# A sliding-window copy: load order of the channel quarters, eight split stores instead of twelve, one tile for each store buffer

## Chip, cores, metric

One core of one Trainium2 chip; the other cores are idle. The metric is the device time of one execution in microseconds (us), lower is better. Fast runs have a granted clock of 1.0; ratios use fast runs alone. The span of the profile is about 1.8 us shorter than the device time.

## The reference, cut to what matters

```python
x: (16, 64, 64, 64) float32; window 8, stride 4; n_h = n_w = 15
for i in range(15):
    for j in range(15):
        result[:, i, j] = x[:, :, 4*i : 4*i + 8, 4*j : 4*j + 8]   # (16, 15, 15, 64, 8, 8)
```

There is no arithmetic, only movement: 16.78 MB are read, 58.98 MB are written.

## The kernel before

The image is held in `L` on 128 partitions: partition = batch (16) x channel half (2) x quarter of the rows (4), 32 channels in each. A "window" is one column j and one slot s of the four row positions in a quarter; ScalarE (ACT) gathers its 8x8 patches into a buffer, and GpSimd (POOL) stores the buffer with one indirect DMA of 128 rows of 8 KB. For s = 3 the patch crosses into the next partition, so VectorE (DVE) does it with a copy and a shuffle, and one row in four has no place in the output (its index is out of range).

To start storing while loads still run, the first windows are split: their first 16 channels are stored as soon as the first half of the channels is loaded (rows of 4 KB), the others later.

```python
    NCH = 4
    cw = CL // NCH
    for k in range(NCH):                    # 4 parts of the channels x 4 quarters = 16 loads of 1 MB
        for q in range(HQ):
            (nc.sync, nc.scalar)[q % 2].dma_start(
                out=L[q::HQ, k * cw : (k + 1) * cw, :, :],
                in_=x_v[q, :, k * cw : (k + 1) * cw, :])
    # ... cut: index tiles idx, idx_last, idx_h, idx_hlast (h: half rows; last: s = 3)
    UNITS = 18                              # half buffers
    G = gpool.tile([P, UNITS * HCL, WS, WS], f32, name="G")

    def window(j, s, half):
        # ... cut: u, n = place and number of half buffers, cs = the channels
        g = G[:, u * HCL : (u + n) * HCL, :, :]
        if not last:
            nc.scalar.copy(out=g, in_=L[:, cs, s * ST : s * ST + WS, cols])
        else:
            nc.vector.tensor_copy(out=g[:, :, 0:ST, :], in_=L[:, cs, s * ST : RB, cols])
            nc.vector.stream_shuffle(out=g[:, :, ST:WS, :], in_=L[:, cs, 0:ST, cols], mask=nxt)
        st = nc.gpsimd.indirect_dma_start(out=o, out_offset=..., in_=g..., ...)

    EARLY = 12
    for j, s in order[:EARLY]:
        window(j, s, 0)                     # first halves
    while late:                             # then 2 second halves, 2 whole windows, ...
        for w in late[:2]: window(*w, 1)
        for w in rest[:2]: window(*w, None)
        late, rest = late[2:], rest[2:]
    for w in rest: window(*w, None)
```

Of the kernel before, what the change touches and what calls it, by code (L numbers as in the profile page):

```python
# [1 line left out]

# [4 lines left out]


@with_exitstack  # L10
def kernel(
    ctx: ExitStack,
    tc: tile.TileContext,
    x: bass.AP,
    window_size: int,
    stride: int,
    out: bass.AP,
):
    nc = tc.nc
    P = nc.NUM_PARTITIONS  # L20

    B, C, H, W = x.shape
    Bo, NH, NW, Co, WSo, WSo2 = out.shape
    WS = int(window_size)
    ST = int(stride)
    assert Bo == B and Co == C and WSo == WS and WSo2 == WS

    f32 = mybir.dt.float32
    i32 = mybir.dt.int32
    ALU = mybir.AluOpType  # L30
    HQ = 4
    CH = P // (B * HQ)
    CL = C // CH
    RB = H // HQ
    NSLOT = RB // ST
    NWIN = NH * NW
    CFREE = CL * WS * WS
    assert HQ == 4 and CH == 2 and WS == 2 * ST

    lpool = ctx.enter_context(tc.tile_pool(name="lpool", bufs=1))  # L40
    ipool = ctx.enter_context(tc.tile_pool(name="ipool", bufs=1))
    gpool = ctx.enter_context(tc.tile_pool(name="gpool", bufs=1))


    L = lpool.tile([P, CL, RB, W], f32)
    x_v = x.rearrange("b (ch cl) (hq r) w -> hq (b ch) cl (r w)", ch=CH, hq=HQ)
    NCH = 4
    cw = CL // NCH
    for k in range(NCH):
        for q in range(HQ):  # L50
            (nc.sync, nc.scalar)[q % 2].dma_start(
                out=L[q::HQ, k * cw : (k + 1) * cw, :, :],
                in_=x_v[q, :, k * cw : (k + 1) * cw, :],
            )


    def itile(name):
        return ipool.tile([P, 1], i32, name=name)

    pi, tb, tq, tc_, idx, idx_last = (itile(n) for n in ("pi", "tb", "tq", "tc", "idx", "idx_last"))  # L60
    nc.gpsimd.iota(pi[:, :], pattern=[[0, 1]], base=0, channel_multiplier=1)  # L61
    nc.vector.tensor_scalar(out=tb[:, :], in0=pi[:, :], scalar1=3, scalar2=None, op0=ALU.logical_shift_right)  # L62
    nc.vector.tensor_scalar(out=tc_[:, :], in0=pi[:, :], scalar1=2, scalar2=1, op0=ALU.logical_shift_right, op1=ALU.bitwise_and)  # L63
    nc.vector.tensor_scalar(out=tq[:, :], in0=pi[:, :], scalar1=HQ - 1, scalar2=None, op0=ALU.bitwise_and)  # L64
    nc.vector.tensor_scalar(out=tb[:, :], in0=tb[:, :], scalar1=float(NWIN * CH), scalar2=None, op0=ALU.mult)  # L65
    nc.vector.tensor_tensor(out=tb[:, :], in0=tb[:, :], in1=tc_[:, :], op=ALU.add)  # L66
    nc.vector.tensor_scalar(out=tc_[:, :], in0=tq[:, :], scalar1=float(NSLOT * NW * CH), scalar2=None, op0=ALU.mult)  # L67
    nc.vector.tensor_tensor(out=idx[:, :], in0=tb[:, :], in1=tc_[:, :], op=ALU.add)  # L68

    nc.vector.tensor_scalar(out=tq[:, :], in0=tq[:, :], scalar1=float(HQ - 1), scalar2=float(2 * B * NWIN * CH), op0=ALU.is_equal, op1=ALU.mult)  # L70
    nc.vector.tensor_tensor(out=idx_last[:, :], in0=idx[:, :], in1=tq[:, :], op=ALU.add)  # L71


    HCL = CL // 2
    idx_h, idx_hlast = itile("idx_h"), itile("idx_hlast")
    for d, e in ((idx_h, idx), (idx_hlast, idx_last)):
        nc.vector.tensor_scalar(out=d[:, :], in0=e[:, :], scalar1=2.0, scalar2=None, op0=ALU.mult)  # L77
    o_v = out.rearrange("b i j (ch cl) r w -> (b i j ch) (cl r w)", ch=CH)
    o_h = out.rearrange("b i j (ch cl) r w -> (b i j ch) (cl r w)", ch=2 * CH)
    nxt = [min(p + 1, 31) for p in range(32)]  # L80


    UNITS = 18
    G = gpool.tile([P, UNITS * HCL, WS, WS], f32, name="G")
    at = 0

    def window(j, s, half):
        nonlocal at
        cols = slice(j * ST, j * ST + WS)
        last = s == NSLOT - 1  # L90
        if half is None:
            n, c0 = 2, 0
            at += at % 2
        else:
            n, c0 = 1, half * HCL
        u = at % UNITS
        at += n
        cs = slice(c0, c0 + n * HCL)
        g = G[:, u * HCL : (u + n) * HCL, :, :]
        if not last:  # L100
            nc.scalar.copy(out=g, in_=L[:, cs, s * ST : s * ST + WS, cols])  # L101
        else:
            nc.vector.tensor_copy(out=g[:, :, 0:ST, :], in_=L[:, cs, s * ST : RB, cols])  # L103
            nc.vector.stream_shuffle(out=g[:, :, ST:WS, :], in_=L[:, cs, 0:ST, cols], mask=nxt)  # L104
        if half is None:
            o, ix = o_v, (idx_last if last else idx)
        else:
            o, ix = o_h, (idx_hlast if last else idx_h)
        st = nc.gpsimd.indirect_dma_start(  # L109
            out=o,  # L110
            out_offset=bass.IndirectOffsetOnAxis(ap=ix[:, 0:1], axis=0),
            in_=g.rearrange("p c r w -> p (c r w)"),
            in_offset=None,
            element_offset=(s * NW + j) * CH * CFREE + (half or 0) * HCL * WS * WS,
            bounds_check=B * NWIN * CH * (1 if half is None else 2) - 1,
            oob_is_err=False,
        )
        tc.declare_no_dep(st.ins, group="stores", reason="each store writes rows of its own")
        tc.add_to_no_dep_group("stores", st.ins)

    order = [(j, s) for j in range(NW) for s in range(NSLOT)]
    EARLY = 12
    for j, s in order[:EARLY]:
        window(j, s, 0)
    late = list(order[:EARLY])
    rest = list(order[EARLY:])
    while late:
        for w in late[:2]:
            window(*w, 1)
        for w in rest[:2]:  # L130
            window(*w, None)
        late, rest = late[2:], rest[2:]
    for w in rest:
        window(*w, None)


# [1 line left out]
_INS = ['x', 'window_size', 'stride']  # L138
_OUTS = [((16, 15, 15, 64, 8, 8), 'float32')]

_NUMBERS = {'window_size': 8, 'stride': 4}


# [26 lines left out]
```

## Time and profile before

| | before |
|---|---|
| device time, median of 6 runs | 194.41 us (194.27 to 194.75) |
| span of the profile | 192.4 us |
| ACT, POOL, DVE busy | 45%, 37%, 16% of the span |
| first store issued; last load landed | 27.4 us; 49.6 us |
| last data of the faster eight DMA engines; of the slower eight | 184.9 us; 188.6 us |

Read the last two rows as the two ends of the DMA work: before the first store only loads move, and after about 184.9 us half of the DMA engines have nothing left. The rows "landed" and "last data" are from the completion records of the transfers: each store counts a semaphore up sixteen times, once per engine. For the last store, the eighth and the sixteenth count are the ends of the two halves. The lines of the profile are shown in the prediction.

One more line of the page of before is that of a half store: how many, and the median time from issue to landing.

```profile
out_dram<-G,idx_h POOLq DMA_INDIRECT x18, 13.6
```

A half store takes about 1.2 us of the engines' time; 13.6 us means that it stands in a queue behind other work.

### The profile page before, as it was taken

The numbers are of one execution on the slowest core, as the hardware profiler recorded it, in microseconds if no ns is written. First come the engines' busy times: TensorE is split into PE (matmuls) and PEld (weight loads), VectorE is DVE, ScalarE is ACT, GpSimd is POOL, SyncE is SP. The second block draws the span as 40 slices with busy tenths as digits, with TensorE's granted clock in tenths as the row PEclk, the third lists the DMA queues.
The fourth block names the chain that finished last, engine by engine and source line by source line (L and its number), as shares of the span: only waits on it lengthen the run. The fifth ranks groups of instructions, "written<-read, shape, count | busy, mean of one in ns | idle before, by whom it ended". The sixth has DMA issues, their size and how long they took to land.

```text
span 192.4 us, 478 instructions
## 1 busy us (share of the span) xinstructions
DVE 30.4 (16%) x65; ACT 86.2 (45%) x55; POOL 70.3 (37%) x77
## 2 busy tenths in 40 slices
DVE  2000050000232302303030122121121203030000
ACT  0000049500699875373747465646565655600000
POOL 0000027723367766456363253434343434440000
DMA  5999999999999999999999999999999999999960
GB/s 183 418 413 410 410 410 414 417 417 422 420 421 427 429 414 429 404 403 418 412 409 409 419 404 409 416 405 409 409 412 409 409 411 412 407 409 414 424 257 17
DMA packets 14724, 75.80 MB, mean 394 GB/s; under 512 B 1984, under 2 KB 1984, under 8 KB 8960
## 3 DMA queue, kind: packets, MB, share of 16 engines
q0 software_dynamic: 10368, 58.99, 75.3%
q1 hardware_dynamic: 2176, 8.39, 11.0%
q10 hardware_dynamic: 2176, 8.39, 10.8%
q14 instruction: 4, 0.03, 0.0%
HBM read 16.78 MB, written 62.91 MB: 414 GB/s over the span
## 4 chain that ended last, share of the span: by engine, by line
DMA 65%; issue 19%; ACT 3%; POOL 1%; POOLq 1%; PEldq 0%
DMA out_dram<-G,idx_last 38%; DMA out_dram<-G,idx 14%; DMA out_dram<-G,idx_h 8%; DMA out_dram<-G,idx_hlast 6%; ACT G L101 3%; POOL out_dram L109 1%; POOLq L165 1%; POOLq L109 0%; POOL pi L61 0%; PEldq L165 0%
## 5 line engine op out<-in xcount | busy, mean ns | idle before, releaser
L101 ACT COPY G<-L 128x2048 f32<-128x2048 f32 (+1 forms) x54 | 84.9, 1613 | 54.4 <-DMA out_dram<-G,idx 18.6
L109 POOL DMA_INDIRECT out_dram<-G,idx x36 | 34.8, 966 | 47.0 <-DMA out_dram<-G,idx 43.1
L103 DVE COPY G<-L 128x1024 f32<-128x1024 f32 (+1 forms) x18 | 11.1, 618 | 138.3 <-DMA out_dram<-G,idx 62.8
L109 POOL DMA_INDIRECT out_dram<-G,idx_h x18 | 17.4, 966 | 13.9 <-DMA out_dram<-G,idx_hlast 4.3
L104 DVE STREAM_SHUFFLE G<-L 128x1024 f32<-128x1024 f32 (+1 forms) x18 | 19.6, 1090 | 0.0
L109 POOL DMA_INDIRECT out_dram<-G,idx_hlast x6 | 5.9, 990 | 27.9 <-DVE G L104 26.4
L109 POOL DMA_INDIRECT out_dram<-G,idx_last x12 | 11.8, 986 | 11.7 <-DVE G L104 6.8
L101 ACT ACT_TABLE_LOAD x1 | 1.3, 1283 | 26.6 <-DMA L<-in_x_dram 26.6
L62 DVE TENSOR_SCALAR tb<-pi 128x1 int32<-128x1 int32 x1 | 0.2, 155 | 1.0 <-POOL pi L61 1.0
L61 POOL IOTA pi<- 128x1 int32 x1 | 0.1, 120 | 0.4 <-PEq L165 0.4
L104 DVE LOAD_MASK_SELECT G<-L x18 | 0.2, 14 | 0.0
L151 POOL MEMSET const-float32-0.0<- 128x1 f32 x1 | 0.1, 100 | 0.2 <-issue 0.2
L68 DVE CUSTOM_DVE_ANT_0 idx<-tb,tc 128x2 uint16<-128x2 uint16 x1 | 0.2, 160 | 0.0
L66 DVE CUSTOM_DVE_ANT_0 tb<-tb,tc 128x2 uint16<-128x2 uint16 x1 | 0.2, 159 | 0.0
L67 DVE TENSOR_SCALAR tc<-tq 128x1 int32<-128x1 int32 x1 | 0.2, 154 | 0.0
L77 DVE TENSOR_SCALAR idx_hlast<-idx_last 128x1 int32<-128x1 int32 x1 | 0.2, 154 | 0.0
L77 DVE TENSOR_SCALAR idx_h<-idx 128x1 int32<-128x1 int32 x1 | 0.2, 154 | 0.0
L71 DVE CUSTOM_DVE_ANT_0 idx_last<-idx,tq 128x2 uint16<-128x2 uint16 x1 | 0.2, 153 | 0.0
L65 DVE TENSOR_SCALAR tb<-tb 128x1 int32<-128x1 int32 x1 | 0.2, 152 | 0.0
L70 DVE TENSOR_SCALAR tq<-tq 128x1 int32<-128x1 int32 x1 | 0.1, 148 | 0.0
L64 DVE TENSOR_SCALAR tq<-pi 128x1 int32<-128x1 int32 x1 | 0.1, 145 | 0.0
L63 DVE TENSOR_SCALAR tc<-pi 128x1 int32<-128x1 int32 x1 | 0.1, 144 | 0.0
(3 smaller groups left out, 0.3 us busy)
## 6 DMA issues: line engine op xcount, KB each, us to landing
L<-in_x_dram ACTq DMA_DIRECT2D x8, 1024.0 KB, 21.1
L<-in_x_dram SPq DMA_DIRECT2D x8, 1024.0 KB, 19.8
out_dram<-G,idx POOLq DMA_INDIRECT x36, 18.2
out_dram<-G,idx_h POOLq DMA_INDIRECT x18, 13.6
out_dram<-G,idx_last POOLq DMA_INDIRECT x12, 18.3
out_dram<-G,idx_hlast POOLq DMA_INDIRECT x6, 13.1
```

The lines of the kernel that those rows point to most:

```text
L62: nc.vector.tensor_scalar(out=tb[:, :], in0=pi[:, :], scalar1=3, scalar2=None, op0=ALU.logical_shift_right)
L65: nc.vector.tensor_scalar(out=tb[:, :], in0=tb[:, :], scalar1=float(NWIN * CH), scalar2=None, op0=ALU.mult)
L66: nc.vector.tensor_tensor(out=tb[:, :], in0=tb[:, :], in1=tc_[:, :], op=ALU.add)
L67: nc.vector.tensor_scalar(out=tc_[:, :], in0=tq[:, :], scalar1=float(NSLOT * NW * CH), scalar2=None, op0=ALU.mult)
L68: nc.vector.tensor_tensor(out=idx[:, :], in0=tb[:, :], in1=tc_[:, :], op=ALU.add)
L71: nc.vector.tensor_tensor(out=idx_last[:, :], in0=idx[:, :], in1=tq[:, :], op=ALU.add)
L77: nc.vector.tensor_scalar(out=d[:, :], in0=e[:, :], scalar1=2.0, scalar2=None, op0=ALU.mult)
L101: nc.scalar.copy(out=g, in_=L[:, cs, s * ST : s * ST + WS, cols])
L103: nc.vector.tensor_copy(out=g[:, :, 0:ST, :], in_=L[:, cs, s * ST : RB, cols])
L104: nc.vector.stream_shuffle(out=g[:, :, ST:WS, :], in_=L[:, cs, 0:ST, cols], mask=nxt)
L109: st = nc.gpsimd.indirect_dma_start(out=o, out_offset=bass.IndirectOffsetOnAxis(ap=ix[:, 0:1], axis=0), in_=g.rearrange("p c r w -> p (c r ...
L165: with _tile.TileContext(nc) as tc:
```

## The change

The intent: with fewer split stores there are fewer small packets and fewer instructions; since one quarter (third of four, not needed by the first half) is loaded ahead, the first half stores start later, and only one quarter of the loads is left to be covered by them. Separate tiles make each store buffer a tile of its own for the dependency tracking.

```diff
-    for k in range(NCH):
+    for k in (2, 0, 1, 3):
...
-    G = gpool.tile([P, UNITS * HCL, WS, WS], f32, name="G")
+    G = [gpool.tile([P, 2 * HCL, WS, WS], f32, name=f"G{n}") for n in range(UNITS // 2)]
...
-        g = G[:, u * HCL : (u + n) * HCL, :, :]
+        g = G[u // 2][:, u % 2 * HCL : (u % 2 + n) * HCL, :, :]
...
-    EARLY = 12
+    EARLY = 8
```

More of the change, by code (lines that the diff above doesn't have):

```diff
@@ L80 @@
     nxt = [min(p + 1, 31) for p in range(32)]
+    order = [(j, s) for j in range(NW) for s in range(NSLOT)]
     UNITS = 18
-    G = gpool.tile([P, UNITS * HCL, WS, WS], f32, name="G")
+    G = [gpool.tile([P, 2 * HCL, WS, WS], f32, name=f"G{n}") for n in range(UNITS // 2)]
     at = 0
@@ L119, in window @@
         tc.add_to_no_dep_group("stores", st.ins)
-    order = [(j, s) for j in range(NW) for s in range(NSLOT)]
-    EARLY = 12
+    EARLY = 8
     for j, s in order[:EARLY]:
```

## The prediction

> **What bounds the kernel now.** I read the slices of the span first, then the stretches, then the waits and the order in time. The slices say which resource is full:
>
> ```profile
> DMA  5999999999999999999999999999999999999960
> GB/s 183 418 413 410 410 410 414 417 417 422 420 421 427 429 414 429 404 403 418 412 409 409 419 404 409 416 405 409 409 412 409 409 411 412 407 409 414 424 257 17
> ...
> q0 software_dynamic: 10368, 58.99, 75.3%
> q1 hardware_dynamic: 2176, 8.39, 11.0%
> q10 hardware_dynamic: 2176, 8.39, 10.8%
> ```
>
> No slice from the second to the thirty-eighth is below 403 GB/s: loads run into stores with no hole. The bytes are 8.39 + 8.39 = 16.78 MB of loads and 58.99 MB of stores, 75.77 MB. At 411 GB/s that is 184.4 us. The first packet starts at about 2.3 us (packet records), so even full DMA engines would end at 186.7 us; the last packet ends at 188.3 us in those records, and some 4 us of completion and closing follow to the span's 192.4. The stretches show the tail and a small difference in rate (columns: stretch, length, DVE, ACT and POOL busy, clock, DMA share, GB/s):
>
> ```profile
> 2.30:30.00 27.70, 3.00 (x10) 3.40 (x4) 2.08 (x2) 1.00 1.02 405
> 30.00:50.00 20.00, 0.20 (x1) 6.75 (x8) 9.66 (x10) 1.00 1.03 418
> 50.00:80.00 30.00, 7.56 (x16) 24.90 (x18) 18.60 (x19) 1.00 1.02 421
> 80.00:100.00 20.00, 3.99 (x9) 11.29 (x6) 10.66 (x12) 1.00 1.02 410
> 100.00:182.00 82.00, 14.47 (x22) 39.86 (x21) 28.96 (x30) 1.00 1.01 411
> ```
>
> Compute is far from full everywhere. The waits agree: the engines wait for DMA stores to give buffers and completion slots back, which is back-pressure from a full DMA, not a cause of the time.
>
> ```profile
> DVE G L103 <- DMA out_dram<-G,idx: 62.8, 9, 8.8
> POOL out_dram L109 <- DMA out_dram<-G,idx: 44.6, 28, 2.3
> ...
> ACT G L101 <- DMA out_dram<-G,idx: 18.6, 19, 3.8
> ```
>
> So the time is start (2.3) + bytes over rate + tail. Only three things can move it: a hole in the DMA stream, the rate, the tail.
>
> **What the Trainium skill says.** "DMA: Bandwidth & Descriptors", section "Issuing engines are not separate DMA queues", says transfers from every issuing engine interleave on the same 16 DMA engines. The trace agrees: 418 GB/s in 30 to 50 us with loads and stores together, no more than with either alone (405 to 421). So starting stores earlier gains nothing while loads fill the engines. The same page, "Queues, rings and completion order", has each engine round-robin between queues packet by packet. The packet records agree roughly: from 30 to 40 us the two load queues move 164 GB/s each and the store queue 89. "HBM Reference", "Specifications", gives about 358 GB/s as a core's share but says a core alone measures well above (about 425); 411 here agrees with the latter, and I see no headroom over the 421 already reached. Last, "DMA: Bandwidth & Descriptors", "Latency and other measured facts", says engines 7 and 15 are usually slower. The trace differs: by the completion records eight of the sixteen fall behind; they are 0.4 us late around 80 us, 2 us at 109 us, 4.1 us on the last store. That is the tail: 320, 201 and 107 GB/s in the last three pairs of microseconds from 183 to 189.
>
> **The change part by part.**
>
> *Load order 2, 0, 1, 3.* What the first stores need now lands with the twelfth load instead of the eighth. The order of before is
>
> ```profile
> 20.70 0.61 ACTq L51 DMA_DIRECT2D L<-in_x_dram  x1
> ...
> 21.98 0.60 SPq L51 DMA_DIRECT2D L<-in_x_dram  x1
> ...
> 25.82 0.61 ACTq L51 DMA_DIRECT2D L<-in_x_dram  x1
> 26.01 0.43 DVE L103 COPY G<-L 128x512 f32<-128x512 f32 x1 [23.66 <-DMA L<-in_x_dram]
> 26.36 0.01 DVE L104 LOAD_MASK_SELECT G<-L  x1
> 26.36 0.71 DVE L104 STREAM_SHUFFLE G<-L 128x512 f32<-128x512 f32 x1
> ...
> 27.36 1.12 POOL L109 DMA_INDIRECT out_dram<-G,idx_hlast  x1 [26.41 <-DVE G L104]
> ```
>
> The eighth load lands at 25.8 (landing records) and the first store is issued 1.5 us later. On each of the two load queues a load takes 5.1 us (issues 20.70 and 25.82), so loads 9, 10, 11, 12 land at about 27, 31, 32, 36 us. First store in the new kernel: 36.0 + 1.5 = 37.5 us, 10 us later. By itself this costs no DMA time, since loads fill the engines until 2.3 + 16.78 MB / 0.411 = 43.1 us. The question is whether stores are there by then. In before the first store packet moved at 31.7 us, 4.3 us after the start of its issue (estimate for after: the same). That gives 41.8 us, 1.3 us before the loads run out. Thereafter POOL issues a store each 1.27 us (0.97 busy, 0.30 between). A split store carries 128 x 4096 B = 0.524 MB, so POOL supplies 0.524 / 1.27 = 413 GB/s, just what the engines take; the first two carry 0.39 MB (a quarter of their rows is out of range). Counting work, the engines finish what is ahead of store 2, 3, 4 at 44.1, 45.0, 46.2; their packets can come at 43.1, 44.3, 45.6. The slack is 0.6 to 1.3 us and never negative. Then stores 9 and 10 follow, and from the 11th whole stores of 1.05 MB per 1.27 us build the backlog up by over 1 us each. The last load should land at 44 to 45 us (49.6 before), so second-half copies start 5 us sooner: ACT makes a half in 1.0 us and a whole in 1.9, or 1.05 MB per 1.9 us = 550 GB/s, also ahead of the DMA. Expected hole: none, with up to 1 us if the 4.3 us is longer.
>
> *8 split in place of 12.* Stores go from 72 to 68 (24 half and 48 whole to 16 and 52). POOL saves 4 x 0.97 and ACT about 0.1 us per pair of halves; all beside the DMA, worth nothing on the path. On the DMA, 960 packets of 4 KB become 480 of 8 KB (less the out-of-range ones). By packet records a 4 KB packet takes 159 ns and an 8 KB one 309 to 316, so 960 x 159 - 480 x 312 = 2.9 us over 16 engines = 0.2 us saved. Against it: stretches with mixed halves and wholes ran at 418 to 421, whole stores alone at 409 to 411. About 8 MB (4 early halves, 4 late, 4 wholes between them) move from the mixed to the whole stretch: 8 MB x (1/410 - 1/420) = 0.5 us lost, if the halves are the reason for the rate. Loads overlapping with stores (418 against 411) shrink by some 12 us: 12 x 1.7% = 0.2 us.
>
> *One tile for each store buffer.* The bytes of buffer are the same, 18 half units, and the buffer waits are already on the particular stores in either version; waits here are shadowed by the DMA. I give it 0.
>
> Sum: -0.2 + 0.5 + 0.2, and 0.2 for the chance of a small hole, is +0.7 us. I halve the two rate terms, as the slow half of the engines set in at about 80 us, when halves were still being stored, which speaks against packet size as the cause. That leaves -0.2 + 0.35 + 0.2 = +0.3, roughly nothing: 194.5 us against 194.4.
>
> **The rivals.** *A hole at 40 to 48 us.* For it: the slack is under 1.5 us, POOL's supply of halves equals the demand, and the first two are short. Against: the 4.3 us was seen behind full load queues and is likely shorter where they thin out, so slack should grow. If store latency were 3 us longer, about 2 to 3 us are lost: 197. *Balance of the engines.* The last half of the engines ends 4 us after the other. If the new order removes the drift, half of it, 2 us, returns: 192.5. If whole stores cause it, starting them 20 us sooner adds some 20 x 2 / 80 = 0.5 us. I see no part of the change that aims at this. *A real gain from later stores*, say by reads and writes not mixing: the rate of the mixed stretch (418) is no lower than that of pure loads, so the profile speaks against it.
>
> **Range and chances.** Start, bytes and tail are common to both, so most of the 194.4 cannot move; the open terms are a hole (0 to 3 us) and the tail (minus 2 to plus 1). Hence 192.6 to 197.0 eight times in ten. Faster by over 2% needs 190.5, more than removing the whole imbalance: 5%. Slower by over 2% needs 198.3, a hole of 4 us: 7%. Within 2%: 88%.
>
> **What would show it.** First store at about 37.5 us; last load at 44 to 45; no slice near 40 to 50 us below about 395 GB/s; the last store's engines again spread over about 4 us; 1920 store packets of 4 KB (15/16 of 16 x 128) instead of 2880. A dip in those slices with ACT or POOL waiting there makes the first rival right; a tail without the slope from 183 to 189 us makes the second right. If the time moves by over 1 us with neither, my account of the rates is wrong.

## The result, and the profile after

The kernel after takes 194.59 us (median of 6 runs, 194.38 to 194.76) against 194.41: ratio 1.0007, 95% interval 0.9994 to 1.002. Ratios here and below are the mean time of one kernel's fast runs over the mean of the other's fast runs of the same rounds, so not quite the ratio of the medians that are quoted.

The stretches of the kernel after, in the same form as those of before (stretch, length, busy times, clock, DMA share, GB/s):

```profile
2.30:30.00 27.70, 0.05 (x1) 0.00 (x0) 0.00 (x0) 1.00 1.02 406
30.00:50.00 20.00, 4.62 (x12) 11.28 (x11) 9.79 (x10) 1.00 1.03 413
50.00:80.00 30.00, 5.57 (x10) 23.72 (x15) 19.74 (x21) 1.00 1.02 419
80.00:100.00 20.00, 3.78 (x6) 11.38 (x6) 7.72 (x8) 1.00 1.01 414
100.00:182.00 82.00, 15.20 (x24) 39.84 (x21) 28.98 (x30) 1.00 1.01 410
```

ACT and POOL did nothing at all before 30 us (columns "x0"), where they had made and issued stores before; the DMA column hardly moves: 413 for 418 from 30 to 50 us, 414 for 410 from 80 to 100. The order in time shows the new start:

```profile
36.11 0.43 DVE L106 COPY G<-L 128x512 f32<-128x512 f32 x1 [33.76 <-DMA L<-in_x_dram]
...
37.46 1.12 POOL L112 DMA_INDIRECT out_dram<-G,idx_hlast  x1 [36.51 <-DVE G L107]
...
45.78 16.58 ACT L104 COPY G<-L 128x1024 f32<-128x1024 f32 x12 [2.65 <-DMA L<-in_x_dram]
```

The first store is issued at 37.46 us in place of 27.36, its first packet moves at 41.8 us (packet records), and the last load lands at 45.6 us, so ACT's wait for the second half is 2.65 us instead of 13.25. Where the old and the new stores meet, the supply holds:

```profile
40.00:43.00 3.00, 0.00 (x0) 3.00 (x4) 2.23 (x3) 1.00 1.03 414
43.00:46.00 3.00, 0.18 (x1) 0.35 (x2) 2.39 (x3) 1.00 1.03 415
46.00:50.00 4.00, 2.44 (x6) 4.00 (x4) 3.08 (x4) 1.00 1.03 422
```

But the page of the kernel after shows how near it came:

```profile
out_dram<-G,idx_h POOLq DMA_INDIRECT x12, 7.1
```

A half store lands 7.1 us after its issue instead of 13.6: there is much less in the queue ahead of it. And the end is as it was, with the slower eight engines 4.2 us behind the others (184.9 and 189.1 us):

```profile
183.00:185.00 2.00, 0.00 (x0) 0.00 (x0) 0.00 (x0) 1.00 0.77 320
185.00:187.00 2.00, 0.00 (x0) 0.00 (x0) 0.00 (x0) 1.00 0.49 209
187.00:189.00 2.00, 0.00 (x0) 0.00 (x0) 0.00 (x0) 1.00 0.36 152
```

So nothing moved. The question for the experiments: do the parts each do nothing, or do they cancel? And what is the tail, the one thing besides bytes that is left?

### The profile page after: what moved, and what is told of

Its sections match the earlier page's. It is cut to its first block, busy times and chain, and to the rows that moved or that the text cites. A ratio compares the mean times of both kernels' runs of the same rounds, so it can differ in the third digit from the quotient of the medians.

```text
span 192.7 us, 457 instructions
## 1 busy us (share of the span) xinstructions
DVE 30.4 (16%) x62; ACT 86.2 (45%) x52; POOL 66.6 (35%) x73
## 4 chain that ended last, share of the span: by engine, by line
DMA 58%; issue 25%; ACT 3%; POOL 3%; POOLq 1%; ACTq 0%; PEldq 0%
DMA out_dram<-G,idx_last 47%; DMA out_dram<-G,idx 7%; DMA out_dram<-G,idx_h 4%; ACT G L104 3%; POOL out_dram L112 3%; POOLq L167 1%; POOLq L112 0%; POOL pi L62 0%; ACTq L104 0%; PEldq L167 0%
## 5 line engine op out<-in xcount | busy, mean ns | idle before, releaser
L112 POOL DMA_INDIRECT out_dram<-G,idx x39 | 37.9, 972 | 51.1 <-DMA out_dram<-G,idx 47.3
L112 POOL DMA_INDIRECT out_dram<-G,idx_last x13 | 12.5, 965 | 12.8 <-DVE G L107 7.8
L112 POOL DMA_INDIRECT out_dram<-G,idx_hlast x4 | 4.0, 1006 | 37.4 <-DVE G L107 36.5
L112 POOL DMA_INDIRECT out_dram<-G,idx_h x12 | 11.8, 980 | 3.7 <-issue 2.4
```

What stands on the lines that cost most here:

```text
L112: st = nc.gpsimd.indirect_dma_start(out=o, out_offset=bass.IndirectOffsetOnAxis(ap=ix[:, 0:1], axis=0), in_=g.rearrange("p c r w -> p (c r ...
```

## The experiments

Eleven kernels ran; the kernel before ran beside each set (medians 194.23 to 194.45). An overview of the first ones, with the two ends taken from the completion records, and the time from which the slower eight engines lag by more than 0.3 us (from the eighth to the ninth completion of a store):

```
run               us      ratio to before  fast end  slow end  lag from
before            194.41                   184.9     188.6     87 us
after             194.59  1.0007           184.9     189.1     79
e1 load order     195.24  1.0040           185.0     189.7     77
e2 EARLY = 8      196.49  1.0104           187.2     191.2     70
e3 tiles          194.40  1.0000           184.8     188.9     91
e4 half last      201.28  1.0350           191.9     195.9     76
e5 7/8            197.50  1.0186           187.7     191.9     67
e6 EARLY = 30     198.02  1.0189           186.5     191.8     81
e9 EARLY = 6      194.59  1.0013           185.3     189.3     77
```

### The parts alone: e1, e2, e3

e1 is the kernel before with only

```diff
-    for k in range(NCH):
+    for k in (2, 0, 1, 3):
```

> The kernel before with the load order alone changed (12 split, one tile). Theory that DMA is full from start to end: first store issued at about 37.5 us instead of 27.4, and the time unchanged, 194.4 within 0.5. Rival that parts of the change cancel: later stores alone cost a hole of 1 to 2 us between 40 and 50 us, so 195.4 to 196.4.

Measured: 195.24 us, ratio 1.0040 (1.0026 to 1.0054). The first store came at 37.5 us as expected, but the time is not unchanged: +0.8 us, between the theory's band and the rival's. The hole that the rival asked for is not there (419 GB/s from 43 to 56 us). The loss is small and spread: 413 for 418 GB/s from 30 to 50 us, 415 for 421 from 56 to 80, and the slow end is 1.1 us later.

e2 is the kernel before with only

```diff
-    EARLY = 12
+    EARLY = 8
```

> The kernel before with 8 split stores in place of 12 and nothing else. Theory (DMA full): 194.4 to 194.9, the slow half of the engines drifting some microseconds sooner so that the last store's completions spread 4.3 us in place of 4.1. Rival that fewer splits gain and the load order eats it: 193 to 193.9. With stores from 27 us on and only 8 halves ready until the loads end near 49 us, a hole could open here near 45 us as well: then a slice under 395 GB/s.

Measured: 196.49 us, ratio 1.0104 (1.0088 to 1.0119). The last sentence of the expectation is what happened. The order in time of POOL in e2:

```profile
36.46 0.96 POOL L109 DMA_INDIRECT out_dram<-G,idx_h  x1 [0.30 <-issue]
51.41 1.20 POOL L109 DMA_INDIRECT out_dram<-G,idx_h  x1 [13.98 <-ACT G L101]
```

and its stretches there, against 421 GB/s in before from 43 to 56 and from 56 to 80 us:

```profile
50.00:52.00 2.00, 1.87 (x6) 1.91 (x3) 0.59 (x1) 1.00 1.04 424
52.00:55.00 3.00, 0.98 (x1) 3.00 (x3) 2.39 (x3) 1.00 0.81 325
55.00:80.00 25.00, 5.21 (x9) 21.02 (x15) 17.59 (x19) 1.00 1.01 397
```

With the old load order eight halves, begun at 27 us, are all issued by 37.4. The loads of the second half land at 49.9 us, and POOL has nothing to issue for 14 us. The eight halves last until the loads end, but not until the next stores' packets come: 325 GB/s from 52 to 55 us. After that the rate stays low, 397 up to 80 us. Compared with before this is 13 us x (421 - 396) / 421 = 0.8 us from 43 to 56 us and 24 us x (421 - 398) / 421 = 1.3 us from 56 to 80, together 2.1 us, where the clock says +2.0.

The engines are not waiting in that second part: their share is 1.01 (1.02 in before), but by the packet records of 56 to 80 us a 4 KB packet takes 170 ns and an 8 KB one 326, against 159 and 312 in before. So after a thin supply the packets themselves are slower for a while; why, no run here shows.

e3 is the kernel before with only the tiles:

```diff
-    G = gpool.tile([P, UNITS * HCL, WS, WS], f32, name="G")
+    G = [gpool.tile([P, 2 * HCL, WS, WS], f32, name=f"G{n}") for n in range(UNITS // 2)]
-        g = G[:, u * HCL : (u + n) * HCL, :, :]
+        g = G[u // 2][:, u % 2 * HCL : (u % 2 + n) * HCL, :, :]
```

> The kernel before with one tile for each store buffer and nothing else. Theory: waits in the shadow of DMA, 194.4 within 0.3. Rival that the single tile's dependencies cost something: under 194.0, and shorter waits of ACT on DVE and of DVE on ACT.

Measured: 194.40 us, ratio 1.0000 (0.9986 to 1.0014). The tiles do nothing.

So the parts are not each neutral: +0.8, +2.0 and 0.0 us alone, and +0.2 together. Fewer halves need the later start (else they run out before the second half is there). With the later start, fewer halves are the better choice (e1 against the kernel after); why is argued under e6.

### How near the late start is to a hole: e4, e5

e4 is the kernel after with the first half loaded third and fourth:

```diff
-    for k in (2, 0, 1, 3):
+    for k in (2, 3, 0, 1):
```

> The kernel after, but the first half loaded third and fourth of four, so that nothing can be stored before all loads have landed (44 to 46 us). Theory: loads run out near 43 us, first store issued near 46.5, its packets near 48 to 51, so a hole of 5 to 8 us and 200 to 202 us, with one or two slices far below 400 GB/s at 43 to 51. Rival that the time of the first store doesn't matter at all (later stores run faster or the tail shrinks): under 197.

Measured: 201.28 us, ratio 1.0350 (1.0335 to 1.0366), as the theory had it. One detail was wrong: two half stores went out at 27 and 29 us, because the scheduler put forward two stores of the second half, which is now loaded first. They were gone long before the hole:

```profile
43.00:45.00 2.00, 0.00 (x0) 0.00 (x0) 0.00 (x0) 1.00 1.03 412
45.00:50.00 5.00, 2.02 (x6) 3.44 (x4) 1.82 (x2) 1.00 0.24 96
50.00:57.00 7.00, 1.91 (x3) 7.00 (x7) 5.40 (x6) 1.00 0.87 344
```

96 GB/s for 5 us is a nearly empty DMA; then POOL, which issues one half per 1.27 us, is behind the engines. By the rates of e4 and of the kernel after, 43 to 56 us (262 for 423 GB/s) costs 4.9 us, 56 to 80 (390 for 416) 1.5 us and 80 to 100 (405 for 414) 0.4 us: 6.8 us, where the medians differ by 6.7.

e5 puts the first half at seven of eight parts:

```diff
-    NCH = 4
+    NCH = 8
-    for k in (2, 0, 1, 3):
+    for k in (4, 5, 6, 0, 1, 2, 3, 7):
```

> The kernel after with loads of half the size, in an order that completes the first half as the seventh of eight parts. Theory of a thin margin: first store at 41 to 42.5 us, its first packet 3 to 4.3 us later, some 2 to 3 us after the loads run out, so a hole of 2 to 3 us in 43 to 48 and 196.3 to 198, between the kernel after (no hole) and the run with the first half last (201.3). Rival that there is slack to spare in the start of the stores: under 195.3.

Measured: 197.50 us (197.26 to 198.7), ratio 1.0186 (1.0163 to 1.0209). The first store was issued at 41.2 us, 3.8 us later than in the kernel after, and the time is 2.9 us longer by the medians. The stretches and the page's line for the halves:

```profile
46.00:50.00 4.00, 0.97 (x3) 4.00 (x4) 3.05 (x4) 1.00 0.92 366
50.00:56.00 6.00, 0.93 (x1) 6.00 (x5) 4.51 (x5) 1.00 0.98 381
...
out_dram<-G,idx_h POOLq DMA_INDIRECT x12, 4.5
```

How long a half store takes without a queue is shown by e4: on the emptied engines its packets began 1.5 us after the issue (47.9 to 49.4) and it landed after 3.3 us. The 3.7 to 4.8 us of the half stores issued up to 53 us in e5 are thus almost no queue. The kernel after, at 7.1 us, has by this estimate nearly 4 us of queue in hand; the kernel before had 10 (13.6). The first packet of e5 came 2.3 us after its issue (43.5 us), not 3 to 4.3. What the expectation had wrong is the form of the loss. There is no empty slice but a supply about a tenth too thin (382 for 423 GB/s from 43 to 56 us, 1.3 us lost) and again a lower rate after it (399 for 416 to 80 us, 1.0 us lost; 408 for 414 to 100 us, 0.3). That adds up to 2.6 of the 2.9 us. The loads of e5 are also half as large, which the edit could not avoid; up to 43 us this cost little (403 for 406 GB/s to 30 us, 411 for 410 from 30 to 43).

### Fewer and more splits: e9, e6

e9 is the kernel after with EARLY = 6, e6 the kernel before with EARLY = 30.

> The kernel after with 6 split stores in place of 8. Loads land at 45.6 us, the second half can be stored from about 47 us, just when the sixth half store has been issued (45.2). Theory (DMA full as long as stores are in the queue): 194.3 to 195.2, no slice under 390 GB/s. Rival: the sequence 12, 8 shows a gain from fewer splits with this load order (195.2, 194.6), so 6 gives about 194.2 or less. Third: a hole near 50 us like that of 8 splits with the old order: 196.

Measured: 194.59 us, ratio 1.0013 (1.0001 to 1.0026): as the theory had it, no hole (424 GB/s from 43 to 56 us), no further gain. From 12 to 8 halves with the late start there are 0.65 us, from 8 to 6 none.

> The kernel before with 30 split stores, so that halves and wholes are mixed to the very end (90 stores). If packets of 8 KB make eight engines fall behind: the last store's completions spread less than 2 us and 191.5 to 193.5. If the drift has nothing to do with the size: spread still about 4 us, and 194 to 195, a little more for the 9 ns and the completion of each extra packet.

Measured: 198.02 us, ratio 1.0189 (1.0176 to 1.0202). Both readings of the expectation were too low. The drift is larger (5.3 us between fast and slow end). Packets of 8 KB are not needed for it: up to 81 us the stores of e6 are all of 4 KB, and from 72 to 80 us their packets already take 166 ns, where they took 159 from 43 to 72. And 18 more split windows cost 3.7 us. The rate falls late in the kernel, not early (it was 419 GB/s from 43 to 72 us):

```profile
72.00:80.00 8.00, 0.00 (x0) 5.82 (x5) 6.17 (x7) 1.00 1.02 398
...
100.00:182.00 82.00, 14.26 (x27) 42.11 (x29) 40.45 (x42) 1.00 1.01 402
```

against 418 from 72 to 80 us and 411 from 100 to 182 in before. From 100 to 182 us that is 82 us x (411 - 402) / 411 = 1.8 of the 3.7 us. In that stretch the packet records give a mean of 166.7 ns for 4 KB and 326.3 ns for 8 KB, and before has 321.2 ns for 8 KB. Two packets of 4 KB thus take 333 ns where one of 8 KB takes 321 in before: 4% more, of which 1.6% is that the 8 KB packets of e6 are slower too. Early, from 50 to 70 us, a 4 KB packet takes 159 ns and an 8 KB one 309 ns, and halves cost little. Halves that are stored after the engines have begun to lag seem to be the dear ones. That fits e1 (halves until 97 us, lag from 77) against the kernel after (halves until 77, lag from 79), but it is argued from these records and was not tried by itself.

### What the tail is: e8, e10, e11, e12

e8 is the kernel after with two of four late whole stores as plain copies from the SyncE queue:

```diff
... cut: o_s, a view of the output by batch and channel half
+        if half is None and s < 2 and j >= 4:
+            for q in range(HQ):
+                st = nc.sync.dma_start(out=o_s[:, :, q * NSLOT + s, j, :],
+                                       in_=g[q::HQ].rearrange("p c r w -> p (c r w)"))
... cut: the stores are declared independent of one another
+            return
```

> The kernel after with two of four late whole stores issued from the SyncE queue as plain copies (four of 32 partitions each) instead of indirect ones from GpSimd. If the drift of eight engines belongs to the stores that GpSimd issues: it grows at about half the rate after 80 us, last completions spread about 2 us, 193 to 194. If it belongs to writing in general: spread about 4 us, 194.3 to 195.5. The plain copies may instead hold up SyncE or wait for one another: then over 196 and a hole.

Measured: 242.54 us (median of six; two of them are slow, and the four fast ones are 240.99 to 242.78), ratio 1.2447 (1.2418 to 1.2476): the last case. The queue of SyncE waited 74.6 us for ACT, ACT for buffers held by stores; with holes of 5 to 6 us and rates near 320 GB/s between them the drift of the kernel cannot be read from it. The completions of its last store lie within 0.1 us, but engines that wait can catch up. Inconclusive for the tail.

e10 is the kernel after, where three of the last stores leave out some partitions (index out of range), which shifts the ends of the engines that would have carried them. Its output is wrong, which doesn't matter for the time.

```diff
... cut: idxA, idxB, lastA, the index tiles in which the rows left out are out of range
+        if j == NW - 1 and s > 0:
+            ix = (idxB, idxA, lastA)[s - 1]
```

In B the partitions whose number has the bit of value 4 are left out, in A those from 64.

> Wrong on purpose, to find which engines are the slow eight: the kernel after, but of its last three stores (last column) the second leaves out partitions whose bit of value 4 is set (store with s = 1), and the last two leave out partitions 64 to 127 (s = 2, 3). If the slow eight carry partitions 0 to 63: the last data end near 189 us as before, and those of 64 to 127 near 178 to 180. If they carry 64 to 127: the fast ones end last, near 185, the slow ones near 182 to 184. If they are every second engine: among the completions of the last store four late and four early in each half.

The time, one run of 194.46 us, says nothing. The sixteen completions of the last four stores, in order, do (us; the eight faster first):

```
s=0 (all rows)        177.6 177.7 177.7 177.7 177.7 177.7 177.8 178.2 | 182.0 182.1 182.1 182.1 182.1 182.2 182.3 182.4
s=1 (without p & 4)   177.8 177.8 177.9 178.4 180.1 180.1 180.2 180.3 | 182.3 182.3 182.4 182.5 184.5 184.5 184.5 184.8
s=2 (without p >= 64) 177.9 178.0 178.1 178.6 180.3 180.3 180.4 180.5 | 184.6 184.6 184.7 184.8 186.9 186.9 187.0 187.2
s=3 (without p >= 64) 178.1 178.2 178.2 178.7 180.4 180.5 180.5 180.6 | 186.5 186.5 186.5 186.7 188.8 188.8 188.8 189.1
```

At s = 1 four engines of each half skip the whole store (177.8, 182.3: hardly any time passes) and four do all of it (+2.4 us). No engine does a part of it. At s = 2 and s = 3 the faster eight do nothing (180.3 becomes 180.5 and 180.6) and the slower eight do all of it (+2.3, then +1.9 where a quarter of the rows has no place). So the slower eight engines are exactly those of partitions 0 to 63. The Trainium skill, "DMA: Bandwidth & Descriptors", section "The descriptor swizzle", gives engine = 8 x (partition >> 6) + ((partition >> 2) & 7) for a transfer to 128 partitions. If it holds for stores too, a skip by the bit of value 4 empties every second engine and a skip of 64 to 127 empties engines 8 to 15. The trace does not number the engines, but it agrees: four of each half are idle at s = 1, and all of one half at s = 2.

e11 makes use of that. In the kernel before, for one late window, the rows of partitions 0 to 63 are copied by ACT into partitions 64 to 127 of another buffer and stored from there. That takes 8 packets from each of the slower engines and gives 8 to each of the others.

```diff
... cut: low = BIG for partitions under 64; idx_up = idx + low; idx_mv = idx_up - (B // 2) * NWIN * CH
+        if part == "mv":
+            nc.scalar.copy(out=g[P // 2 :], in_=L[: P // 2, cs, s * ST : s * ST + WS, cols])
...
+        if w == (NW - 2, 1):
+            window(*w, None, "up")     # partitions 64 to 127 only
+            window(*w, None, "mv")     # the rows of 0 to 63, from 64 to 127
```

> The kernel before, with the rows of partitions 0 to 63 of one late store (last column but one, s = 1) copied to partitions 64 to 127 and stored from there, so that the slow eight engines carry 8 packets of 8 KB less and the other eight 8 more. If the tail is the imbalance of the engines: slow end 188.6 - 2.5 = 186.1, fast end 184.9 + 2.5 = 187.4, so about 1.2 us less: 193.2, correct result, completions of the last store spread about 1.3 us. Rival that the time is set by the total rate, and the slow ones are slow because the fast ones run: 194.4 again.

Measured: correct, 192.92 us (192.87 to 192.93), ratio 0.9931 (0.9917 to 0.9944). The slope at the end has gone:

```profile
183.00:185.00 2.00, 0.00 (x0) 0.00 (x0) 0.00 (x0) 1.00 1.02 422
185.00:187.00 2.00, 0.00 (x0) 0.00 (x0) 0.00 (x0) 1.00 0.69 283
187.00:189.00 2.00, 0.00 (x0) 0.00 (x0) 0.00 (x0) 1.00 0.00 0
```

Both halves end at 186.8 to 187.3 us.

e12 is the same edit on the kernel after.

> The same move in the kernel after: slow end 189.0 - 2.5 = 186.5, fast end 184.8 + 2.5 = 187.3, so about 1.7 us less than the kernel after: 192.9. Rival as in the run beside it: 194.6.

Measured: correct, 192.86 us (192.70 to 192.92), ratio to before 0.9929 (0.9916 to 0.9943), last completion at 187.3 us. Both versions beat before, beside which they ran, by 0.7%, and so the kernel after too; between them there is nothing to choose. That the tail is work left over on one group of engines, and not a limit of the whole, is shown by this. The group is not slow when it is alone: in before an 8 KB packet takes 309 ns from 56 to 72 us, ahead of the lag, 321 from 100 to 182, and 309 again from 185 us, when the slower eight alone still work.

## Why the prediction was right

**The bound.** The prediction said that the time is start, bytes over rate, and tail, with the DMA full throughout. Shown: every run that moved the time did it through a stretch with the DMA below its rate (e2, e4, e5, e8, and e1 by a little), a lower rate late (e6) or the tail (e11, e12); compute was idle up to 36 us in the kernel after at no cost.

**The load order.** Its dates were right to within 0.6 us for the last load, and closer for the rest: twelfth load and first store at 36.0 and 37.5 us predicted, 35.9 and 37.46 measured; first store packet 41.8 predicted and measured; last load 44 to 45 predicted, 45.6 measured. No hole, 0.2 us lost by less overlap of loads and stores: 413 for 418 GB/s over 20 us is 0.24 us. The slack of "0.6 to 1.3 us" fits e5, which issued 3.8 us later and lost 2.9; but e5 lost it by a thin supply and slower packets, not by a hole, so it does not test that figure. That the 4.3 us shrink where the loads thin out was right: 2.3 us in e5, 1.5 us on the idle engines of e4. Yet alone this part costs 0.8 us (e1), where the working has 0.1 to 0.2 for the rate and 0.2 for a chance of a hole.

**The splits.** The prediction valued 8 in place of 12 by packets, 0.2 us saved. Over all packets of the stores the records have 143.87 us per engine before and 143.78 after, so 0.1. But the step "worth nothing on the path" hid a condition that the prediction did not see: with the old load order the same step costs 2.0 us (e2), since eight halves end before the loads do, and with the new one it saves 0.65 us (e1 against after). The working gave the splits -0.2 + 0.25 us and the load order about +0.3; the runs give +0.8 for the load order (e1) and then -0.65 for the splits. The dates and the absence of a hole were worked out for both parts together and were right by their mechanism; that these two terms, each off by half a microsecond or more, cancel to +0.2 is luck. This is the step that would have failed for either part alone. The packets of 4 KB are the 1920 that it named.

**The rate terms.** 0.5 us was set against the change "if the halves are the reason for the rate", then halved. e6 shows the halves are not a gain: 30 splits run at 402 GB/s where 12 run at 411. The reading under it does not hold in the profile of before either: from 80 to 100 us 575 packets of 4 KB moved beside 712 of 8 KB, so that stretch was mixed, and it ran at 410. The kernel after, with whole stores alone, runs 414 there. The lower rate goes with slower packets, which came in every run of the table, in e6 with 4 KB alone. Against the gain stands the slow end, 0.4 us later, with a lag from 79 instead of 87 us; that the one offsets the other is argued, not shown.

**Slips.** The terms add up to +0.35, which is 194.7 and not 194.5; the result lies between. From 30 to 40 us the packet records give 159 and 163 GB/s for the two load queues and 94 for the stores, not 164 and 89; the reading stands.

**The tiles.** 0 predicted, 1.0000 measured.

**The rivals.** The hole is real, and sits just beside the new kernel on either hand: 8 splits with the early start (196.5 us) or a start 3.8 us later (197.5 us). The balance rival was rightly put down as a gain of about 2 us that no part of this change aims at; e11 and e12 took 1.3 and 1.7 us of it. Its other half, 0.5 us more of tail "if whole stores cause it", has the size of the slow end's 0.4 us, but e6 speaks against that cause: its packets slow down before the first one of 8 KB.

**Open.** Why the engines of partitions 0 to 63 fall behind, what sets the time at which the lag begins (67 to 91 us in these runs), and why packets are slower late and after a thin supply (390 to 399 GB/s up to 80 us, with the engines busy).

## What to carry to other kernels

When the transfer engines are full from start to end, do not ask what a change saves on compute engines but whether work will always be queued: compare, store by store, when the engines run out with when the next packets arrive. Two settings that share such a margin (when stores may start, and how many small ones are ready) must be judged together, since one of them changed alone can open a hole (e2). Look also at the completions of the last transfer engine by engine: a spread there is time that moving a few rows can win back.

## What the Trainium skill lacked or had wrong

- "DMA: Bandwidth & Descriptors", "Latency and other measured facts": it names engines 7 and 15 as usually slower. Here eight engines, those of partitions 0 to 63 in indirect stores from GpSimd, lag by 3.7 to 5.3 us at the end of 190 us (e10 shows which), and shifting 8 packets per engine gained 0.7% (e11, e12).
- The same page has no figure for how long after issue an indirect store's first packet moves while loads fill the engines: 4.3 us here, from 27.4 to 31.7 us before and from 37.5 to 41.8 us after; 1.5 us on idle engines (e4).
- No page has what a small row costs beside a large one late in a run of stores: 166.7 ns for 4 KB and 326.3 ns for 8 KB in e6, against 159 and 309 ns early in before. Nor has any that packets of one size slow down in the course of a kernel whose engines stay busy (8 KB in before: 309 ns from 56 to 72 us, 321 from 100 to 182).
